# One-hot tiles with two tokens side by side instead of eight, in the dense expert weights of a two-model block

## The chip, the cores and the metric

The kernel runs on one core of a Trainium2 chip. The metric is the device time of one execution in microseconds. The kernel before took 4570.91 us, the median of three runs (4564.49 to 4579.38).

## The reference

Two models run one after the other on 256 tokens of 1024 features. The first has two layers, and each layer ends in product-key experts (`_peer`); layer 0 runs them on two streams, the context and x, and layer 1 on x alone. For one token the experts are:

```
s      = query . keys, for 8 heads and two halves: 128 scores each
v, i   = top 16 of each half;  cand = the 16 x 16 sums;  sc, pos = top 16 of cand
g      = softmax(sc);  expert = i1 * 128 + i2
out    = sum over 8 heads x 16 ranks of g * gelu(h . U[expert]) * V[expert]
```

A token therefore chooses 128 of 16384 experts, and each choice has a first index i1 (0 to 127), a second index i2 (0 to 127) and a weight g. The second model (a gated delta rule layer, a sparse attention layer, memory attention and convolutional feed-forward) does not touch what is changed.

## The kernel before

The experts are computed densely: every expert for every token, with a weight that is zero where the expert was not chosen. The expert tables go by chunks of one first index, 128 chunks in each stream, and the 128 second indices of a chunk lie on partitions.

`peer` (from line 1201) runs two products per chunk. `first()` takes a chunk of U: a DMA into `raw`, a split into two float32r parts `whi` (ScalarE, line 335) and `wlo` (line 338, VectorE or GpSimd), 24 matmuls `ps_U` of 256 columns, and a gelu into a slot of the ring `A`. `second(c)` takes a chunk of V: the slot is split into `a_hi` and `a_lo` (lines 348 and 349), V is split in the same way, and 12 matmuls of 512 columns add to four banks `ps_acc`. U runs ahead of V by the slots of the ring.

Before `second` reads a slot it must be multiplied with the dense weights of that chunk, and this is the work that the change touches, `peer_weights` (from line 1158). One generator makes the weights of n first indices (36, then 46, then 46) for all 256 tokens of a stream, in 32 batches of TB = 8 tokens. A batch is:

- `P2` (line 1180, VectorE): a one-hot of i2 for each of the 128 choices on partitions, 128 columns for each of 8 tokens, float16
- `P1` (line 1183, VectorE): a one-hot of i1, n columns for each of 8 tokens
- `Pg` (line 1184, VectorE): P1 times the two float16 parts of g, both parts in one instruction
- `use` (line 1172, VectorE): the ring's slots times the products of the batch before
- 16 matmuls `ps_G` on TensorE (line 308 through `mm`), two for each token: the token's 128 columns of `P2` are the loaded weights, and the token's n columns of `Pg` are what moves through the array.

There are nine such generators: three ranges for each of the two streams of layer 0 and for the one stream of layer 1, so 288 batches and 4608 matmuls, 1536 of 36 columns and 3072 of 46. The first generator of a layer runs beside `first()` alone, while the ring fills, one chunk of U for each batch. The others run inside the loop over chunks of V, one or two batches in a pass, mostly beside a `first()` and a `second()`. In the last range of a layer U has ended, and a pass is a `second()` with its batches.

The low parts of the split weights go to VectorE or GpSimd by a counter: `pool_each` is 4 in the loop (every fourth on GpSimd), 1 (all on GpSimd) once U has ended and batches are still due, and 1 or 2 while the first generator runs. The order of instructions on each engine is made by the framework's scheduler; the 16 matmuls of a batch stay together. `P1`, `P2` and `Pg` have two buffers each. The tiles lie with the token as the innermost index, so one token's columns stand 8 float16 values apart:

```
P2 = pe.tile([P, P, TB], FH, tag="P2", bufs=2, name="P2")
self.mm(o, P2[:, :, half * HB + t], Pg[:, 0, :, half * HB + t], True, False)
self.mm(o, P2[:, :, half * HB + t], Pg[:, 1, :, half * HB + t], False, True)
```

Of the kernel before, what the change touches and what calls it, by code (L numbers as in the profile page):

```python
# [7 lines left out]
FT = mybir.dt.float32  # L8
FR = mybir.dt.float32r
FH = mybir.dt.float16  # L10
# [14 lines left out]
APART = 2             # layer 0's last tiles of the out-projection that do the context's half first  # L25
OUTB, OUTK = 3, 6     # first tiles of the out-projection that begin with the first OUTK chunks of y
MEMW = 3              # steps between a memory norm's squares and its sum
FRONTW = 5            # the same for the second stream's norm before the choice of experts
NK0 = 2               # steps of attention before the memory's products
GK = 2                # steps of memory attention before the out-projection  # L30
PE1 = range(40, 47)   # steps of the choice of experts beside which Pool makes all the low parts
# chunks whose squares Pool adds up before the sum over partitions, by norm
# [3 lines left out]
# ---------------------------------------------------------------- layout of the inputs (host)  # L36
def fm(a):
    """[T, D] -> [128, D/128, T], feature-major."""
    a = np.asarray(a)
    t, d = a.shape  # L40
    return np.ascontiguousarray(a.reshape(t, d // P, P).transpose(2, 1, 0))


def cols(v):
    """[n*128] -> [128, n]."""
    return np.ascontiguousarray(np.asarray(v).reshape(-1, P).T)


def pack_t(w):
    """[K, C] -> [C/128, 128, K/128 * 128]: column tiles, rows on partitions."""  # L50
    k, c = w.shape
    return np.ascontiguousarray(
        w.reshape(k // P, P, c // P, P).transpose(2, 1, 0, 3)).reshape(c // P, P, k)


def pack_m(w, g):
    """[K, C] -> [K/128/g, 128, g*C]: row chunks, all columns."""
    k, c = w.shape
    n = k // P // g
    return np.ascontiguousarray(w.reshape(n, g, P, c).transpose(0, 2, 1, 3)).reshape(n, P, g * c)  # L60
# [26 lines left out]
# column tiles of w_in, in the order of the array  # L87
T_G16, T_QK, T_V, T_GV, T_O, T_U, T_CV, T_FT, T_GATE = 0, 1, 5, 7, 9, 11, 13, 17, 19
EARLY = (T_G16, T_QK + 2, T_QK + 3, T_QK, T_QK + 1, T_CV + 2)   # the first tiles of w_in
ADA0 = (4, 0)     # the layers' first groups of 512 modulations that aren't made with the first norm  # L90
# [30 lines left out]
def sincos_parts():  # L121
    """Feature-major: half of the features depend on the row alone, half on the column alone."""
    e = fm(sincos())
    return np.ascontiguousarray(np.concatenate([e[:, :4, ::64].reshape(P, 16), e[:, 4:, :64].reshape(P, 256)], axis=1))


def constants():
    """Arrays that depend on shapes alone."""
# [25 lines left out]
    # slices of 40 columns: ones in column j; in columns 8 + j and 32 + j  # L154
# [34 lines left out]
def prep(I):  # L189
    """The arrays as the program reads them: reordered, and padded with zeros."""  # L190
# [14 lines left out]
    # the modulations of the first norm, chunk by chunk of its features: (chunk, half of the rows)  # L205
    A["wadaf"] = np.ascontiguousarray(
        I["w_ada"][0][:, :2 * D].reshape(2, 4, P, 2, KC, P).transpose(4, 0, 2, 1, 3, 5)).reshape(KC, 2, P, 1024)
    for l in range(2):
# [26 lines left out]
        # (branch, half of the columns): [row of 128, (column group, row group, column)]  # L235
# [33 lines left out]
    for i in range(2):  # L269
# [4 lines left out]
        A[f"wom{i}"] = np.ascontiguousarray(      # the memory's rows, two column tiles at a time  # L274
# [7 lines left out]
# ---------------------------------------------------------------- the program  # L282
class Kern:
    def __init__(self, tc, A, L, out):
# [8 lines left out]
        self.pool_each = 4     # GpSimd makes one of so many low parts  # L293
        self.n_ps = 0

    # ---- small things
# [13 lines left out]
    def tr(self, o, x):  # L310
        """o <- x transposed."""
# [17 lines left out]
    def split(self, raw, f=1024, own=None):  # L329
        """float32 -> two float32r parts whose sum it is, to float32's accuracy; own: a pool with tiles for them."""  # L330
# [10 lines left out]
    def weight(self, ap, f=1024, ahead=0, own=None):  # L341
        """ahead: by how many instructions it goes before its place in the program."""
# [3 lines left out]
    def hilo(self, hi, lo, src, copy=None):  # L346
        """hi, lo <- src; src float32 in SBUF."""
# [3 lines left out]
    # ---- constants  # L351
# [23 lines left out]
    def load_x(self, src_x, src_c):  # L375
# [4 lines left out]
        # the mixers' and experts' input: the context's tokens, then x's  # L380
# [15 lines left out]
    # ---- adaLN: mods[l][:, m*8+dc, stream]; streams: 0 the context, 1 x  # L396
    def ada_load_c(self):
# [3 lines left out]
        # silu(c) of both streams, in 32 columns  # L401
# [4 lines left out]
    def ada(self, l, g0, g1, pool):  # L406
        """Generator: column groups g0.. (of 512) of the modulations."""
# [15 lines left out]
    def first_chunks(self, Rs):  # L423
        """The first norm, chunk by chunk of the features as their modulations come, and with every chunk its part
        of the products with the first tiles of w_in, which are returned."""
# [39 lines left out]
    def ada_mm(self, ps, w, j, start, stop):  # L465
        """Each of the four products (half of the features, half of the columns) in its own columns of the array."""
# [15 lines left out]
    def gains(self, l, which):  # L482
        """gain * (1 + scale), for norm 1 or 2."""
# [7 lines left out]
    # ---- RMS norm over features, feature-major  # L491
    def squares(self, x, R=None, added=0):
        """The sum of so many chunks' squares, by GpSimd."""
# [12 lines left out]
    def rstd_bc(self, x, R=None, added=0, begun=False):  # L506
        """[128, NT] with 1/rms of each token in every row; begun: R is the sum of the squares of chunks."""
# [15 lines left out]
    def sqrt_ahead(self, at):  # L523
        """Has ACT load its table for sqrt, when at is there."""
# [3 lines left out]
    def rstd(self, R, ss, n):  # L528
        """R <- 1/sqrt(ss/n + eps)."""
# [3 lines left out]
    def norm(self, x, gain, shift, hi, lo, R=None, ks=range(KC), added=0):  # L533
        """hi, lo <- rmsnorm(x) * gain + shift; gain, shift: chunk -> [128, 1]."""
# [13 lines left out]
    # ---- products with streamed weights  # L548
    def lin_t(self, w, h, t0, t1, ps, nk=KC, k0=0, start=True, stop=True):
        """ps[:, :t1-t0] (+)= W^T h: the tile's 128 columns on partitions."""  # L550
# [7 lines left out]
    # ---- the mixer of the first model's layers  # L558
# [5 lines left out]
    def ctx_ahead(self):  # L564
        """Generator: the next layer's norm of the context, when its experts are done."""
# [6 lines left out]
    def mixer(self, l, side=()):  # L572
# [57 lines left out]
        def merge(i):  # L630
            """ysum += sigmoid(gate) * (z[i] @ w_branch[i]); after the last of them, the two parts of ysum in y."""
# [20 lines left out]
        # ---- mLSTM: gates, as rows in the order of the scan  # L652
        g16 = scratch("g16")[:, :2 * NT]
        nc.scalar.activation(g16, tile_of(T_G16, 0), AF.Identity, bias=lp("gateb"))
        # partitions: 64 * stream + 32 * direction + head
# [26 lines left out]
        # rows: 0 the exponents of the sources, 1 -m, 2 m0 - M (x), the sources' weights in the final state (context)  # L682
# [21 lines left out]
        # -M in two parts, its blocks of tokens 0, 0, 1, 1  # L704
# [4 lines left out]
        # ---- mLSTM: q, k (convolution over tokens, silu)  # L709
# [16 lines left out]
        # ---- mLSTM: v (with a column of ones), and the v of the spatial gating, token-major  # L726
# [30 lines left out]
        # ---- mLSTM: the two directions of every stream  # L757
# [6 lines left out]
        for s in (0, 1):  # L764
# [5 lines left out]
            for h in range(4):  # L770
# [26 lines left out]
                with tc.manual_schedule(engines={mybir.EngineType.PE}):  # L797
                    for d in range(2):
                        # block of targets: (column of Pt, block of sources)
# [5 lines left out]
        # norm over each head, output gate  # L805
# [20 lines left out]
        # ---- convolution branch: gate, and the convolution over tokens  # L826
# [13 lines left out]
        # ---- Fourier branch  # L840
# [5 lines left out]
        for s in streams:  # L846
            y1 = bp.tile([P, 2, 2, 2, P], FT, name="y1") if last else scratch("y1").rearrange(
                "p (b j c e) -> p b j c e", b=2, j=2, c=2)  # block, tile, cos|sin, channel
# [18 lines left out]
        # ---- convolution branch: the convolution over tokens  # L867
# [8 lines left out]
        # ---- spatial gating  # L876
# [42 lines left out]
        # ---- convolution branch  # L919
# [42 lines left out]
        # the last chunks of y come late  # L962
# [7 lines left out]
        # the context is finished first: its experts follow  # L970
# [12 lines left out]
    def ml_state(self, bp, qk, vx, rT, c0):  # L983
        """Final state of the context's scan, both directions: c0[(head%2, dk), dir, head, dv|1], zero in the rows of the other head."""
# [20 lines left out]
    def ml_out(self, bp, s, h, nd, qk, c0f, rT, hs):  # L1005
        """hs[:, block, head] <- the sum of both directions' outputs, token-major."""
        nc = self.nc
        # [token, (direction, block of tokens), dv|1]
# [25 lines left out]
    def advance(self, side, n=1):  # L1034
        """n steps of the generators in side."""
# [5 lines left out]
    # ---- product-key experts: every expert for every token, its weight zero where it isn't chosen  # L1041
    # first indices whose weights are made at a time, and slots of the ring, by the number of streams
    RANGES = {1: (36, 46, 46), 2: (36, 46, 46)}
    RING = {1: 77, 2: 66}
    TB = 8          # tokens in one batch of them
    GS = 16384.0     # the weights' scale in float16

    def peer_open(self, es, ngroups):
# [3 lines left out]
        self.io_t = self.pe.tile([P, P, self.TB], FH, name="io_t")  # L1052
        nc.vector.tensor_copy(self.io_t, iota.unsqueeze(2).broadcast_to([P, P, self.TB]))
# [9 lines left out]
    def peer_front(self, l, s, st):  # L1063
        """Generator: the chosen experts and their weights, slots (head, rank) on partitions."""
# [33 lines left out]
        gT = st["gT"] = pe.tile([P, 2, NT], FH, tag="gT", bufs=self.nh, name="gT")  # L1098
        for b in range(2):
# [43 lines left out]
            nc.scalar.copy(gT[:, 0, ts], ps[:, 2 * P:3 * P])  # L1143
            nc.vector.tensor_sub(gT[:, 1, ts], ps[:, 2 * P:3 * P], gT[:, 0, ts])
# [4 lines left out]
    def top16(self, s, v, i):  # L1149
        """v, i <- the 16 largest of s and their places, in order; s is overwritten."""  # L1150
# [7 lines left out]
    def peer_weights(self, st, A, s0, i0, n):  # L1158
        """Generator: the products of first indices i0..i0+n, in the slots of A from s0 on, times their weights."""
# [15 lines left out]

        for t0 in range(0, NT, TB):
            ts = slice(t0, t0 + TB)
            bc = lambda q, m: st[q][:, ts].unsqueeze(1).broadcast_to([P, m, TB])
            P2 = pe.tile([P, P, TB], FH, tag="P2", bufs=2, name="P2")
# [918 lines left out]
```

## Time and profile before

| What | Value |
|---|---|
| Median of three runs | 4570.91 us (4564.49 to 4579.38) |
| Profiled execution, span from first to last instruction | 4573.1 us; the profile gives no time of its own around the span |
| TensorE matmuls busy | 4452.0 us, 97% |
| VectorE busy | 3040.3 us, 66% |
| ScalarE busy | 2022.9 us, 44% |
| GpSimd busy | 1193.1 us, 26% |
| Mean granted TensorE clock | 0.981 of full speed |

Busy time counts an instruction from its start to its end, also while it is held up by another engine, so a busy VectorE may be waiting. Matmuls overlap: the time that one costs is the distance from its start to the next one's start, not its duration. A granted clock of 1.0 is 2.4 GHz, and 0.5 is 1.2 GHz.

### The profile page before, as it was taken

The numbers are of one execution on the slowest core, as the hardware profiler recorded it, in microseconds if no ns is written. First come the engines' busy times: TensorE is split into PE (matmuls) and PEld (weight loads), VectorE is DVE, ScalarE is ACT, GpSimd is POOL, SyncE is SP. The second block draws the span as 40 slices with busy tenths as digits, with TensorE's granted clock in tenths as the row PEclk, the third lists the DMA queues.
The fourth block names the chain that finished last, engine by engine and source line by source line (L and its number), as shares of the span: only waits on it lengthen the run. The fifth ranks groups of instructions, "written<-read, shape, count | busy, mean of one in ns | idle before, by whom it ended". The sixth has DMA issues, their size and how long they took to land. (4 is left out here: it accounts for less than half of the span.)

```text
span 4573.1 us, 79225 instructions
## 1 busy us (share of the span) xinstructions
PE 4452.0 (97%) x31661; PEld 4029.5 (88%) x31661; DVE 3040.3 (66%) x5528; ACT 2022.9 (44%) x3223; POOL 1193.1 (26%) x591
## 2 busy tenths in 40 slices
PE   8999999999999999999999999999999999999999
PEld 6777999899788888999888999899988889999899
DVE  5743698687765566564756758876757566686685
ACT  5343442534433335334245544334443464654454
POOL 1023354112211112112321234642134212222122
PEclk9999999999999999999999999999999999999999
DMA  5243453544545655446354444444544541456355
GB/s 195 95 159 116 135 160 112 177 130 152 180 164 182 219 184 160 139 135 188 107 170 146 146 153 158 137 144 143 170 157 134 189 141 33 146 185 196 111 167 157
DMA packets 192129, 693.89 MB, mean 152 GB/s; under 512 B 21640, under 2 KB 23312, under 8 KB 191760
## 3 DMA queue, kind: packets, MB, share of 16 engines
q1 hardware_dynamic: 191616, 688.31, 47.1%
q8 instruction: 248, 4.06, 0.4%
q14 instruction: 121, 0.99, 0.1%
q10 hardware_dynamic: 144, 0.52, 0.0%
HBM read 687.69 MB, written 1.06 MB: 151 GB/s over the span
## 5 line engine op out<-in xcount | busy, mean ns | idle before, releaser
L338 POOL TENSOR_TENSOR wlo<-raw,whi 128x1024 fp32r<-128x1024 f32 (+1 forms) x419 | 1034.0, 2469 | 2960.5 <-ACT whi L335 2766.1
L335 ACT CAST whi<-raw 128x1024 fp32r<-128x1024 f32 (+1 forms) x1190 | 1241.8, 1045 | 1192.9 <-PE ps_U L308 374.6
L338 DVE TENSOR_TENSOR wlo<-raw,whi 128x1024 fp32r<-128x1024 f32 (+1 forms) x771 | 958.4, 1244 | 506.0 <-ACT whi L335 494.2
L308 PE MATMUL ps_acc<-whi,a_hi 128*128 128x512 f32 x1536 | 642.5, 418 | 0.0
L308 PE MATMUL ps_acc<-wlo,a_hi 128*128 128x512 f32 x1536 | 625.4, 407 | 3.7 <-DVE wlo L338 2.5
L308 PE MATMUL ps_acc<-whi,a_lo 128*128 128x512 f32 x1536 | 621.1, 406 | 0.6 <-DVE a_lo L349 0.6
L308 PE MATMUL ps_U<-hh_hi,wlo 128*128 128x256 f32 x2048 | 579.9, 283 | 14.1 <-DVE wlo L338 11.7
L308 PE MATMUL ps_U<-hh_hi,whi 128*128 128x256 f32 x2048 | 581.3, 284 | 0.9 <-ACT whi L335 0.9
L308 PE MATMUL ps_U<-hh_lo,whi 128*128 128x256 f32 x2048 | 579.0, 283 | 0.0
L348 ACT CAST a_hi<-A 128x256 fp32r<-128x256 f32 x384 | 156.1, 407 | 863.7 <-PE ps_acc L308 847.7
L308 PE MATMUL ps_G<-Pg,P 128*128 128x46 f16 (+1 forms) x4608 | 425.5, 265 | 4.0 <-DVE Pg L1184 4.0
L349 DVE TENSOR_TENSOR a_lo<-A,a_hi 128x256 fp32r<-128x256 f32 x384 | 203.0, 529 | 335.3 <-ACT a_hi L348 333.0
L308 PEld LDWEIGHTS <-P 128*128 128x128 f16 x4608 | 385.9, 148 | 36.1 <-issue 19.1
L1180 DVE TENSOR_TENSOR P<-io_t,i2T 128x1024 f16<-128x1024 f16 x288 | 404.6, 1405 | 6.7 <-PE ps_G L308 6.7
L308 PEld LDWEIGHTS ps_U<-hh_hi,wlo 128*128 128x128 f32 x2048 | 389.4, 190 | 15.9 <-DVE wlo L338 13.3
L308 PEld LDWEIGHTS ps_U<-hh_hi,whi 128*128 128x128 f32 x2048 | 390.7, 191 | 10.1 <-ACT whi L335 1.1
L308 PEld LDWEIGHTS ps_U<-hh_lo,whi 128*128 128x128 f32 x2048 | 389.6, 190 | 8.4
L308 PEld LDWEIGHTS ps_acc<-whi,a_lo 128*128 128x128 f32 x1536 | 299.0, 195 | 73.0 <-DVE a_lo L349 1.1
L308 PEld LDWEIGHTS ps_acc<-whi,a_hi 128*128 128x128 f32 x1536 | 302.4, 197 | 67.9 <-issue 8.6
L308 PEld LDWEIGHTS ps_acc<-wlo,a_hi 128*128 128x128 f32 x1536 | 300.3, 195 | 65.7 <-DVE wlo L338 3.3
L308 PE MATMUL ps_U<-h_hi,wlo 128*128 128x256 f32 x1024 | 291.9, 285 | 10.0 <-DVE wlo L338 7.6
L308 PE MATMUL ps_U<-h_hi,whi 128*128 128x256 f32 x1024 | 294.6, 288 | 0.9 <-ACT whi L335 0.9
(610 smaller groups left out, 9305.1 us busy)
## 6 DMA issues: line engine op xcount, KB each, us to landing
raw<-in_U SPq DMA_DIRECT2D x384, 512.0 KB, 3.7
raw<-in_V SPq DMA_DIRECT2D x384, 512.0 KB, 3.7
raw<-in_win SPq DMA_DIRECT2D x96, 512.0 KB, 3.8
raw<-in_wup SPq DMA_DIRECT2D x88, 512.0 KB, 3.8
raw<-in_wada SPq DMA_DIRECT2D x80, 512.0 KB, 4.5
raw<-in_wq SPq DMA_DIRECT2D x48, 512.0 KB, 3.7
raw<-in_gwin SPq DMA_DIRECT2D x37, 512.0 KB, 3.7
raw<-in_wdn SPq DMA_DIRECT2D x32, 512.0 KB, 4.4
```

What stands on the lines that cost most here:

```text
L308: self.nc.tensor.matmul(o, l, r, start=start, stop=stop)
L335: nc.scalar.copy(hi[:, :f], raw[:, :f])
L338: eng.tensor_sub(lo[:, :f], raw[:, :f], hi[:, :f].bitcast(FT))
L348: (copy or self.nc.scalar.copy)(hi, src)
L349: self.nc.vector.tensor_sub(lo, src, hi.bitcast(FT))
L1180: nc.vector.tensor_tensor(P2, self.io_t, bc("i2T", P), op=OP.is_equal)
```

## The change

The one-hot tiles keep their 8 tokens per batch, but they hold them as four groups of two: the group is the outermost index, then the 128 (or n) columns, then the two tokens (TQ = 2). One token's columns now stand 2 float16 values apart, for `P2` and for `Pg`. The constant `io_t` holds two copies of each number instead of eight and is read again for each group. The tile of g (`gT`) is laid out batch by batch so that it can be read in groups of two. `Pg` is made by two instructions, one for each part of g, instead of one. Number, order and sizes of the matmuls stay. Comments are removed throughout, without effect on the program.

```diff
     TB = 8
+    TQ = 2
-        self.io_t = self.pe.tile([P, P, self.TB], FH, name="io_t")
-        nc.vector.tensor_copy(self.io_t, iota.unsqueeze(2).broadcast_to([P, P, self.TB]))
+        self.io_t = self.pe.tile([P, P, self.TQ], FH, name="io_t")
+        nc.vector.tensor_copy(self.io_t, iota.unsqueeze(2).broadcast_to([P, P, self.TQ]))
...
-        gT = st["gT"] = pe.tile([P, 2, NT], FH, tag="gT", bufs=self.nh, name="gT")
+        gT = st["gT"] = pe.tile([P, NT // self.TB, 2, self.TB], FH, tag="gT", bufs=self.nh, name="gT")
...
-            nc.scalar.copy(gT[:, 0, ts], ps[:, 2 * P:3 * P])
-            nc.vector.tensor_sub(gT[:, 1, ts], ps[:, 2 * P:3 * P], gT[:, 0, ts])
+            tb = slice(b * P // self.TB, (b + 1) * P // self.TB)
+            gv = ps[:, 2 * P:3 * P].rearrange("p (k t) -> p k t", t=self.TB)
+            nc.scalar.copy(gT[:, tb, 0], gv)
+            nc.vector.tensor_sub(gT[:, tb, 1], gv, gT[:, tb, 0])
...
+        TQ = self.TQ
+        H = TB // TQ
         for t0 in range(0, NT, TB):
             ts = slice(t0, t0 + TB)
-            bc = lambda q, m: st[q][:, ts].unsqueeze(1).broadcast_to([P, m, TB])
-            P2 = pe.tile([P, P, TB], FH, tag="P2", bufs=2, name="P2")
-            nc.vector.tensor_tensor(P2, self.io_t, bc("i2T", P), op=OP.is_equal)
-            P1 = pe.tile([P, self.RG, TB], FH, tag="P1", bufs=2, name="P1")[:, :n]
-            Pg = pe.tile([P, 2, self.RG, TB], FH, tag="Pg", bufs=2, name="Pg")[:, :, :n]
-            nc.vector.tensor_tensor(P1, self.io_t[:, i0:i0 + n], bc("i1T", n), op=OP.is_equal)
-            nc.vector.tensor_tensor(Pg, P1.unsqueeze(1).broadcast_to([P, 2, n, TB]),
-                                    st["gT"][:, :, ts].unsqueeze(2).broadcast_to([P, 2, n, TB]), op=OP.mult)
+            bc = lambda q, m: (st[q][:, ts].rearrange("p (h t) -> p h t", h=H).unsqueeze(2)
+                               .broadcast_to([P, H, m, TQ]))
+            io = lambda j, m: self.io_t[:, j:j + m].unsqueeze(1).broadcast_to([P, H, m, TQ])
+            P2 = pe.tile([P, H, P, TQ], FH, tag="P2", bufs=2, name="P2")
+            nc.vector.tensor_tensor(P2, io(0, P), bc("i2T", P), op=OP.is_equal)
+            P1 = pe.tile([P, H, self.RG, TQ], FH, tag="P1", bufs=2, name="P1")[:, :, :n]
+            Pg = pe.tile([P, 2 * H, self.RG, TQ], FH, tag="Pg", bufs=2, name="Pg")[:, :, :n]
+            nc.vector.tensor_tensor(P1, io(i0, n), bc("i1T", n), op=OP.is_equal)
+            gt = st["gT"][:, t0 // TB].rearrange("p q (h t) -> p (q h) t", t=TQ)
+            for q in range(2):
+                nc.vector.tensor_tensor(Pg[:, q * H:(q + 1) * H], P1,
+                                        gt[:, q * H:(q + 1) * H].unsqueeze(2).broadcast_to([P, H, n, TQ]), op=OP.mult)
...
-                        self.mm(o, P2[:, :, half * HB + t], Pg[:, 0, :, half * HB + t], True, False)
-                        self.mm(o, P2[:, :, half * HB + t], Pg[:, 1, :, half * HB + t], False, True)
+                        h, q = divmod(half * HB + t, TQ)
+                        self.mm(o, P2[:, h, :, q], Pg[:, h, :, q], True, False)
+                        self.mm(o, P2[:, h, :, q], Pg[:, H + h, :, q], False, True)
```

## Rows read from the trace of the kernel before

**Rows 1.** First part of the page: busy time, share and instructions by engine.
```profile
PE 4452.0 (97%) x31661; PEld 4029.5 (88%) x31661; DVE 3040.3 (66%) x5528; ACT 2022.9 (44%) x3223; POOL 1193.1 (26%) x591
```

**Rows 2.** Busy time by stretch; columns are stretch, length, engines, granted clock, DMA.
```profile
880.00:1090.00 210.00, 210.00 (x1641) 197.58 (x1641) 163.80 (x452) 78.34 (x124) 37.03 (x14) 1.00 0.46 141
1240.00:1440.00 200.00, 200.00 (x1462) 174.56 (x1458) 122.79 (x207) 63.35 (x96) 26.41 (x11) 0.92 0.51 169
1560.00:1760.00 200.00, 200.00 (x1589) 178.39 (x1588) 141.17 (x244) 75.46 (x113) 33.57 (x14) 1.00 0.56 182
1840.00:2010.00 170.00, 170.00 (x1188) 154.91 (x1188) 107.73 (x192) 55.33 (x82) 25.40 (x11) 0.91 0.42 128
...
2890.00:3050.00 160.00, 152.36 (x1450) 150.78 (x1450) 133.56 (x144) 53.38 (x84) 90.96 (x38) 0.97 0.41 132
3050.00:3290.00 240.00, 239.36 (x1712) 218.75 (x1711) 161.83 (x258) 101.41 (x156) 47.52 (x24) 0.99 0.48 156
```

**Rows 3.** Groups by shape: the 46-column products of the one-hot tiles.
```profile
L308 PE MATMUL ps_G<-Pg,P 128*128 128x46 f16 x3072 | 301.2, 271 | 4.0 <-DVE Pg L1184 4.0
```

**Rows 4.** Timeline of TensorE's matmuls: start, duration (us), at three places.
```profile
1416.06 0.28 PE L308 MATMUL ps_U<-hh_hi,wlo 128*128 128x256 f32 x1
1416.18 0.28 PE L308 MATMUL ps_U<-hh_hi,whi 128*128 128x256 f32 x1
...
1419.33 1.65 PE L308 MATMUL ps_G<-Pg,P 128*128 128x46 f16 x16
1420.76 0.48 PE L308 MATMUL ps_acc<-whi,a_hi 128*128 128x512 f32 x1
...
2953.62 1.32 PE L308 MATMUL ps_G<-Pg,P 128*128 128x36 f16 x16
2954.74 0.37 PE L308 MATMUL ps_U<-h_hi,whi 128*128 128x256 f32 x1
```

**Rows 5.** Timeline of TensorE's weight loads: the first two of a batch.
```profile
1419.32 0.14 PEld L308 LDWEIGHTS <-P 128*128 128x128 f16 x1 [0.41 <-issue]
...
1419.36 0.23 PEld L308 LDWEIGHTS <-P 128*128 128x128 f16 x2
```

**Rows 6.** Timeline of TensorE around a fall of the granted clock.
```profile
1399.46 3.05 PE L308 MATMUL ps_G<-Pg,P 128*128 128x46 f16 x32
...
1402.87 0.63 PE L308 MATMUL ps_acc<-wlo,a_hi 128*128 128x512 f32 x1
1403.29 0.63 PE L308 MATMUL ps_acc<-whi,a_lo 128*128 128x512 f32 x1
```

**Rows 7.** Timeline of GpSimd and VectorE while the ring fills, layer 1.
```profile
2954.88 2.40 POOL L338 TENSOR_TENSOR wlo<-raw,whi 128x1024 fp32r<-128x1024 f32 x1 [1.65 <-ACT whi L335]
2955.35 2.47 DVE L1180 TENSOR_TENSOR P<-io_t,i2T 128x1024 f16<-128x1024 f16 x1
...
2958.93 2.39 POOL L338 TENSOR_TENSOR wlo<-raw,whi 128x1024 fp32r<-128x1024 f32 x1 [1.66 <-ACT whi L335]
```

**Rows 8.** Timeline of GpSimd and VectorE after U has ended, layer 1.
```profile
3445.28 2.40 POOL L338 TENSOR_TENSOR wlo<-raw,whi 128x1024 fp32r<-128x1024 f32 x1 [1.90 <-ACT whi L335]
...
3448.99 0.42 DVE L349 TENSOR_TENSOR a_lo<-A,a_hi 128x256 fp32r<-128x256 f32 x1
...
3449.57 2.40 POOL L338 TENSOR_TENSOR wlo<-raw,whi 128x1024 fp32r<-128x1024 f32 x1 [1.88 <-ACT whi L335]
```

**Rows 9.** VectorE's instructions by line: duration in ns, min/median/max, then first and last start.
```profile
L1180 DVE TENSOR_TENSOR P<-io_t,i2T x288: 675/685/2748, 648.8 to 3510.5; 128x1024 f16<-128x1024 f16 x144
L1183 DVE TENSOR_TENSOR P<-io_t,i1T x288: 293/337/2559, 651.0 to 3504.8; 128x368 f16<-128x368 f16 x96, 128x288 f16<-128x288 f16 x48
L1184 DVE TENSOR_TENSOR Pg<-P,gT x288: 443/528/2753, 657.5 to 3512.6; 128x736 f16<-128x736 f16 x96, 128x576 f16<-128x576 f16 x48
...
L1104 DVE TENSOR_TENSOR cand<-vt x24: 672/684/2904, 530.4 to 2865.6; 128x512 f32<-128x512 f32 x24
...
L1125 DVE TENSOR_TENSOR eq<-eq,itf x24: 1200/1221/3436, 613.0 to 2905.5; 128x1024 f16<-128x1024 f16 x24
```

## The prediction

> **What bounds the kernel.** I read the busy shares first: TensorE is at 97% and no other engine above 66% [rows 1], so time is won where TensorE's work shrinks, as long as nothing else is full there. The second view is the table of stretches that hold the generators of expert weights [rows 2]: in the four stretches from 880 to 2010 us TensorE is busy all the time, in the one from 3050 for 239 of 240 us, and VectorE for 63 to 78% of each. Third is the timeline of TensorE's starts, since the distance from start to start is what a matmul costs [rows 4]. Sixteen products of 46 columns go from 1419.33 to 1420.76, 89 ns each, 3072 of them busy for 301 us in all [rows 3]; sixteen of 36 columns from 2953.62 to 2954.74, 70 ns each. Both are 1.94 ns for a column, so it is the moving columns that set the pace and not the weight load, which has 128 columns in either case. The float32r products of 256 columns next to them start 0.12 us apart, 0.47 ns a column [rows 4]. What differs is the distance of columns in memory: 16 bytes for the one-hot tiles, 4 bytes for float32r.
>
> **TensorE.** After the change a token's columns stand 4 bytes apart, like those of float32r. If the pace follows the distance, 46 columns take 46 x 0.47 = 22 ns and 36 take 17. Then the weight load is late next. The first two loads of a batch, which wait for no product, start 39 ns apart [rows 5]; that is with columns 16 bytes apart, so a load costs 39 ns or less. Bounds for a product are 22 ns (the load hides) and the present 89 and 70 (distance does not matter). I take 39, the only measured load. A batch of 46 columns falls from 1.43 to 0.62 us, one of 36 from 1.12 to 0.62: 0.81 and 0.50 us, or 26 and 16 us for a generator of 32 batches.
>
> The Trainium skill (TensorE: Matmul & The Clock Gate, Back-to-back issue gap) puts a stream of pairs of load and matmul at about 81 ns each at 128 columns; as a floor here it would leave 8 ns on the 46-column products and nothing on the others, some 20 us in all. The trace disagrees with it as a floor, for the 36-column pairs already run at 70 ns [rows 4].
>
> **The clock.** The granted clock is 0.92 from 1240 to 1440, 0.91 from 1840 to 2010 and 0.99 from 3050 to 3290 [rows 2]. At one of these falls 32 one-hot products had run for 2.8 us, and the 512-column products behind them start 0.42 us apart [rows 6], 1.2 GHz in place of 2.4. In the stretch from 1560, where the batches have 36 columns, the clock stays at 1.00. After the change even two batches are 1.3 us, little more than the 1.12 of one batch there, so I expect the falls to go: 0.08 x 200 + 0.09 x 170 + 0.01 x 240 = 34 us. At worst they stay and this is nothing.
>
> **VectorE.** Elements stay the same in number; Pg becomes two instructions of the size of P1. That is 2 x 337 against 528 ns [rows 9], 0.15 us more for a batch and 5 us for a generator. What I can't read from a row is an input whose rows hold two float16 values, each row read 128 or n times. Lower bound: 685 ns for P2 as now. Upper bound: the 1221 ns that L1125 takes for as many float16 values where one input repeats single values, one element at a time instead of two [rows 9]. I take no loss, because the nearest row is L1104: it rereads one 4-byte value sixteen times, and 512 of them take 684 ns [rows 9], just what the 512 pairs of P2 take now; a repeated word by itself is not slow.
>
> The Trainium skill speaks against the change here: Vector Engine (DVE) Microarchitecture Reference, section Measured stream behaviour on trn2, says that a port streams at full rate only where its elements come in runs of two or more adjacent 4-byte words (1.05 ns a column; 1.73 where one source hops at each). Two float16 values are one word, so by it P2 would be some 0.35 us longer, an estimate, and a batch 0.72. By L1104, which stays on a word at full rate, this is no hop, and no run here shows the other reading.
>
> **Stretch by stretch.** In the five with U and V, TensorE's saving counts while VectorE still fits:
> - from 880: 26 us; VectorE would have 164 + 5 of 184 us, 92%, and some passes will wait: I count 22
> - from 1240: 26 + 16 for the clock = 42; VectorE 128 of 158
> - from 1560: 16; VectorE 146 of 184
> - from 1840: 26 + 15 = 41; VectorE 112 of 129, so 40
> - from 3050: 26 + 2 = 28; VectorE 167 of 212.
>
> That is 148 us. The other four generators gain little, since there GpSimd makes all low parts, and VectorE's one-hots stand still while it does: P2 takes 2.47 us beside a low part of 2.40 and ends 0.54 after it [rows 7], not its own 0.69. While the ring fills a pass is 4.05 us, from low part to low part [rows 7]. What can't overlap is 2.40 + 0.54 + P1 and Pg at 36 columns (about 0.29 and 0.44, the minima of rows 9) + 0.15 for the split = 3.82. So at most 0.2 us x 64 batches = 13 us is to be had of the 32 that TensorE gives; I take 6. After U has ended a pass is 4.29 us, and the same sum with 46 columns and a_lo (0.42) is 2.40 + 0.54 + 0.34 + 0.53 + 0.15 + 0.42 = 4.38 [rows 8, 9]: nothing gained, at worst 0.1 us x 62 batches = 6 lost. The shorter io_t and the regrouped gT are a handful of instructions outside the loops; nothing.
>
> Sum: 148 + 6 = 154 us. The profiled span is 4573.1 us, 2 us above the median, with nothing recorded around it; 4573 - 154 = 4419, and against the median 4417.
>
> **Rivals.**
> 1. *The load shortens too.* Rows 5 bound it from above only; with columns closer it may reach 25 ns. Another 14 ns x 16 x 160 batches in the five stretches is 36 us, of which VectorE, near 90% in two of them, leaves 25: 4392.
> 2. *GpSimd holds VectorE up.* GpSimd makes every fourth low part in the five stretches too, and holds up VectorE as in rows 7. For it: VectorE at 87 to 92% after the change. Against it: busy time already includes its waits. With half of everything kept, 77 us: 4494.
> 3. *VectorE drops to one element at a time* (slower). If rows of two values don't pair, P2 costs 0.54 us more, P1 0.19 and Pg 0.38, with the split 1.26 us a batch. While the ring fills the sum becomes 4.93 against 4.05, 56 us for 64 batches; after U has ended 5.49 against 4.29, 1.2 x 62 = 74. In the five stretches VectorE then has 204, 163, 181, 143 and 202 us, and the gains shrink to 6, 37, 16, 27 and 28 = 114. Net 16 slower at least, 4587; with the waits of an engine at its limit about 30, 4600. It decides from about 1.15 us more per batch on; below that the kernel is still faster. For it: no row shows an input in rows of two. Against it: L1104 as above.
> By the Trainium skill's rates, as above, the loss would be 0.87 us a batch with the split and the kernel still faster, about 4515, an estimate.
> 4. *The distance is not it* and the pace stays. Then the split alone costs, 9 us where VectorE bounds: 4580. Against it: 1.94 ns a column has no other difference to stand on but the type, and float16 is the narrower one.
>
> **How the numbers follow.** Forecast 0.52 (own range 4395 to 4450), rivals 0.17, 0.15, 0.10 and 0.06. The range takes in the first rival's centre and the second's, 4380 to 4510. What this kernel's measurement can tell from no change is 0.3%, 14 us. Faster 0.52 + 0.17 + 0.15 + 0.02 (the third rival where its price stays under 1.15 us) = 0.86; same 0.05, from the fourth; slower 0.09.
>
> **What would show it.** Sixteen one-hot products from start to the next engine work in 0.6 to 0.7 us, equal for 36 and 46 columns if the load is the bound, and in proportion if not. P2's shortest duration at 0.68 us, half a Pg at 0.34; 1.2 and 0.53 would be rival 3. Granted clock 1.00 in the stretches from 1240 and 1840. Passes of some 3.9 us while the ring fills and 4.3 after U. The forecast is wrong if products still cost 70 ns or more, if VectorE's shares in the five stretches reach 97%, or if the clock falls as often as before.

## The result and the profile after

The changed kernel takes 4386.5 us (median of 4 runs, 4381.2 to 4392.3) against 4567.7 for the kernel before beside it (4558.1 to 4579.4): ratio 0.9608, 95% interval 0.9588 to 0.9628, 181 us faster. The forecast was 4417, its range 4380 to 4510, of which it gave 4395 to 4450 to its own mechanism; the time lies outside that inner range and nearest to the first rival's 4392.

First part of the page of the changed kernel, by engine, to be held against [rows 1]: TensorE is busy for 246 us less, VectorE for 66 more.

```profile
PE 4205.9 (96%) x31661; PEld 3765.4 (86%) x31661; DVE 3106.5 (71%) x5816; ACT 2021.7 (46%) x3223; POOL 1225.9 (28%) x591
```

Groups by shape of the changed kernel, the one-hot products (busy us, mean ns of one, then idle time before them and who ended it). In [rows 3] one took 271 ns and TensorE waited 4 us for `Pg`; now one takes 185 or 180 ns, and TensorE waits 54 us for `Pg` (36.1 + 17.6).

```profile
L308 PE MATMUL ps_G<-Pg,P 128*128 128x46 f16 x3072 | 114.0, 185 | 39.2 <-DVE Pg L1193 36.1 <-ACT a_hi L348 0.4
L308 PE MATMUL ps_G<-Pg,P 128*128 128x36 f16 x1536 | 61.6, 180 | 19.0 <-DVE Pg L1193 17.6
```

TensorE's starts in the changed kernel, two batches of 46 columns and one of 36, each with the work behind it; they answer to [rows 4].

```profile
1259.16 0.98 PE L308 MATMUL ps_G<-Pg,P 128*128 128x46 f16 x32
1259.98 0.47 PE L308 MATMUL ps_acc<-whi,a_hi 128*128 128x512 f32 x1
...
2844.21 0.75 PE L308 MATMUL ps_G<-Pg,P 128*128 128x36 f16 x16
2845.14 0.39 PE L308 MATMUL ps_U<-h_hi,whi 128*128 128x256 f32 x1 [0.18 <-DVE A L1175]
```

Thirty-two products now take 0.82 us, 25.6 ns each. From one start to the next the median is 25 ns for 36 and for 46 columns (71 and 90 before). The second place shows what is late next: the product behind the batch waits 0.18 us for VectorE.

VectorE's instructions by line in the changed kernel (ns, min/median/max), against [rows 9]: `P2` and `P1` have their old medians and, within 11 ns, their old minima; a half of `Pg` is as long as a `P1`.

```profile
L1193 DVE TENSOR_TENSOR Pg<-P,gT x576: 294/337/2559, 655.7 to 3336.8; 128x368 f16<-128x368 f16 x126, 128x288 f16<-128x288 f16 x66
L1187 DVE TENSOR_TENSOR P<-io_t,i2T x288: 664/684/2879, 650.3 to 3333.8; 128x1024 f16<-128x1024 f16 x144
L1190 DVE TENSOR_TENSOR P<-io_t,i1T x288: 295/337/2557, 651.5 to 3329.0; 128x368 f16<-128x368 f16 x96, 128x288 f16<-128x288 f16 x48
```

Busy time by stretch of the changed kernel, columns as in [rows 2], one row for each of the nine generators.

```profile
700.00:805.00 105.00, 86.66 (x997) 82.18 (x997) 93.20 (x152) 27.95 (x42) 52.63 (x22) 0.89 0.31 102
920.00:1063.00 143.00, 140.81 (x1367) 130.26 (x1366) 140.06 (x413) 60.09 (x96) 41.04 (x11) 1.00 0.50 158
1259.00:1381.00 122.00, 120.99 (x1243) 104.03 (x1238) 111.53 (x218) 47.26 (x72) 22.89 (x8) 1.00 0.61 207
1500.00:1677.00 177.00, 177.00 (x1592) 155.29 (x1592) 147.41 (x273) 74.42 (x112) 33.63 (x13) 1.00 0.61 198
1791.00:1902.00 111.00, 110.88 (x1119) 100.84 (x1116) 109.14 (x230) 46.11 (x69) 23.20 (x8) 1.00 0.51 164
2065.00:2166.00 101.00, 79.54 (x722) 57.06 (x721) 92.35 (x166) 25.23 (x36) 44.73 (x18) 0.88 0.31 95
2779.00:2900.00 121.00, 115.21 (x1251) 106.46 (x1251) 119.43 (x150) 41.66 (x63) 79.78 (x32) 1.00 0.41 136
2934.00:3114.00 180.00, 176.90 (x1523) 159.07 (x1522) 158.51 (x274) 86.63 (x135) 45.86 (x21) 0.99 0.53 178
3216.00:3338.00 122.00, 105.48 (x844) 77.58 (x840) 118.83 (x177) 39.01 (x58) 68.94 (x29) 0.97 0.38 125
```

Three things are to be seen. In the stretches from 1259 and 1791 the granted clock is 1.00, where it was 0.92 and 0.91. In those from 920 and 1791 VectorE is busy for 98%. And in the first, sixth and ninth row (a ring fill, and the two after U has ended) TensorE idles for 18, 21 and 17 us, in the first two at a clock of 0.89 and 0.88 (1.00 and 0.92 before): here the gain went.

The time by generator, from the first start of its products to the last, read from the two timelines:

| Stretch (after) | Before, us | After, us | Saved | Forecast |
|---|---|---|---|---|
| 700, ring fills, layer 0 | 94.6 | 104.6 | -10.0 | 6 with the next fill |
| 920 | 171.5 | 142.9 | 28.6 | 22 |
| 1259 | 165.6 | 121.7 | 43.9 | 42 |
| 1500 (36 columns) | 198.9 | 176.4 | 22.5 | 16 |
| 1791 | 156.5 | 111.1 | 45.4 | 40 |
| 2065, U ended, layer 0 | 108.2 | 100.3 | 7.9 | 0 |
| 2779, ring fills, layer 1 | 126.7 | 121.2 | 5.5 | see above |
| 2934 | 209.8 | 179.6 | 30.2 | 28 |
| 3216, U ended, layer 1 | 129.1 | 121.9 | 7.2 | 0 |
| Sum | | | 181.2 | 154 |

### The profile page after: what moved, and what is told of

It is laid out like the page before. It is cut to its first block, busy times and chain, and to the rows that moved or that the text cites. A ratio compares the mean times of both kernels' runs of the same rounds, so it can differ in the third digit from the quotient of the medians.

```text
span 4390.5 us, 79517 instructions
## 1 busy us (share of the span) xinstructions
PE 4205.9 (96%) x31661; PEld 3765.4 (86%) x31661; DVE 3106.5 (71%) x5816; ACT 2021.7 (46%) x3223; POOL 1225.9 (28%) x591
## 5 line engine op out<-in xcount | busy, mean ns | idle before, releaser
L338 POOL TENSOR_TENSOR wlo<-raw,whi 128x1024 fp32r<-128x1024 f32 (+1 forms) x419 | 1068.7, 2552 | 2746.8 <-ACT whi L335 2504.1
L308 PE MATMUL ps_acc<-whi,a_hi 128*128 128x512 f32 x1536 | 629.7, 410 | 0.0
L308 PE MATMUL ps_acc<-wlo,a_hi 128*128 128x512 f32 x1536 | 614.0, 400 | 6.8 <-DVE wlo L338 4.4
L308 PE MATMUL ps_acc<-whi,a_lo 128*128 128x512 f32 x1536 | 609.2, 399 | 0.0
L308 PEld LDWEIGHTS ps_acc<-whi,a_hi 128*128 128x128 f32 x1536 | 291.9, 190 | 65.3 <-issue 9.1
L1193 DVE TENSOR_TENSOR Pg<-P,gT 128x368 f16<-128x368 f16 (+1 forms) x576 | 339.2, 627 | 0.0
L1187 DVE TENSOR_TENSOR P<-io_t,i2T 128x1024 f16<-128x1024 f16 x288 | 308.0, 1070 | 4.6 <-PE ps_G L308 4.6
L308 PE MATMUL ps_U<-h_lo,whi 128*128 128x256 f32 x1024 | 292.1, 285 | 0.0
```

The costliest lines, as they stand in the source:

```text
L308: self.nc.tensor.matmul(o, l, r, start=start, stop=stop)
L338: eng.tensor_sub(lo[:, :f], raw[:, :f], hi[:, :f].bitcast(FT))
L1187: nc.vector.tensor_tensor(P2, io(0, P), bc("i2T", P), op=OP.is_equal)
L1193: nc.vector.tensor_tensor(Pg[:, q * H:(q + 1) * H], P1, gt[:, q * H:(q + 1) * H].unsqueeze(2).broadcast_to([P, H, n, TQ]), op=OP.mult)
```

## The experiments

Ten kernels ran, each beside the kernel before (median 4571.0 in the first four, 4565.5 in the next four, 4568.9 in the last two). The ns given for a product below are medians from the start of one product to the start of the next.

### One operand at a time

**pg_only**: the loaded weights go back to eight tokens side by side (16 bytes apart), the moving columns stay at two tokens.

```diff
-            P2 = pe.tile([P, H, P, TQ], FH, tag="P2", bufs=2, name="P2")
+            P2 = pe.tile([P, P, TB], FH, tag="P2", bufs=2, name="P2")
...
-                        self.mm(o, P2[:, h, :, q], Pg[:, h, :, q], True, False)
+                        self.mm(o, P2[:, :, half * HB + t], Pg[:, h, :, q], True, False)
...
```

> The changed kernel with P2 (what is loaded) back at eight tokens side by side, Pg (what moves) left at two, and still two instructions for Pg. Theory A, load and moving each cost by the distance of their own columns, and a product takes the longest of load, moving and a fixed step of 25 ns: the load alone sets the pace at 39 ns, the gap of the first two loads before the change, for 36 and 46 columns alike. Against the changed kernel 14 ns x 4608 = 65 us of TensorE's time come back, of which VectorE's limit hides some 25: ratio to before 0.965 to 0.972. Rival B, only the moving columns mattered and the load was never in the way: 25 ns and 0.961.

Measured: 4465.9 us, ratio 0.9772 (0.9751 to 0.9793). TensorE's starts in this kernel:

```profile
1304.13 2.14 PE L308 MATMUL ps_G<-Pg,P 128*128 128x46 f16 x32
1306.11 0.48 PE L308 MATMUL ps_acc<-whi,a_hi 128*128 128x512 f32 x1
...
2840.39 1.16 PE L308 MATMUL ps_G<-Pg,P 128*128 128x36 f16 x16
2841.40 0.36 PE L308 MATMUL ps_U<-h_hi,whi 128*128 128x256 f32 x1
```

60 ns for both shapes. Equal paces for 46 and 36 columns mean that the load sets them, as the forecast had it; but a load of 16-byte steps is 60 ns in a stream, not the 39 that lie between the first two (39 here too), and so the kernel is slower than the expected 0.965 to 0.972. Why the first two are closer was not found out.

**p2_only**: the reverse, the loaded weights at two tokens, the moving columns at eight (with `Pg` in one instruction).

```diff
-            Pg = pe.tile([P, 2 * H, self.RG, TQ], FH, tag="Pg", bufs=2, name="Pg")[:, :, :n]
+            Pg = pe.tile([P, 2, self.RG, TB], FH, tag="Pg", bufs=2, name="Pg")[:, :, :n]
...
-                        self.mm(o, P2[:, h, :, q], Pg[:, h, :, q], True, False)
+                        self.mm(o, P2[:, h, :, q], Pg[:, 0, :, half * HB + t], True, False)
...
```

> The changed kernel with Pg (what moves) back at eight tokens side by side and in one instruction, P2 (what is loaded) left at two. Theory A: the moving columns set the pace as before, 89 and 70 ns, the gap of the first two loads falls to 15 ns without use, the clock falls as often as before from 1240 to 1440 us: ratio to before 0.995 to 1.003. Rival C, the load sets the pace: 25 ns and about 0.96.

Measured: 4538.0 us, ratio 0.9924 (0.9898 to 0.9949).

```profile
1299.16 2.88 PE L308 MATMUL ps_G<-Pg,P 128*128 128x46 f16 x32
1301.83 0.48 PE L308 MATMUL ps_acc<-whi,a_hi 128*128 128x512 f32 x1
...
2904.29 1.25 PE L308 MATMUL ps_G<-Pg,P 128*128 128x36 f16 x16
2905.34 0.36 PE L308 MATMUL ps_U<-h_hi,whi 128*128 128x256 f32 x1
```

2.67 us for 32 products and 1.05 for 16; the medians are 85 and 68 ns, nearly in proportion to the columns. The moving operand was the bound, and a shorter load alone is worth 33 us, more than the expected 0.995 to 1.003 allowed. Two things were not in the expectation. The products became 5 and 3 ns shorter, some 20 us in all (an estimate), so that a product is not quite the longest of load and moving alone. And the fifth generator ran at a clock of 0.98 in place of 0.90 and saved 13.5 us; in the third it stayed at 0.91, as expected. Both operands alone give 105 + 33 = 138 us, both together 181: each takes away what the other leaves as the bound.

### Other distances

**tq4**: four tokens side by side, 8 bytes from column to column. **tq1**: one, 2 bytes.

```diff
-    TQ = 2
+    TQ = 4   # tq1: TQ = 1
```

> The changed kernel with four tokens side by side (TQ = 4), columns 8 bytes apart in both tiles. Theory A with a cost in proportion to the distance: 1.94 x 8/16 = 0.97 ns a column, 45 ns for 46 columns and 35 for 36, ratio to before 0.968 to 0.975. Rival D, a distance below 16 bytes is free: 25 ns for both shapes, ratio 0.961. VectorE's instructions keep their durations in both.

> The changed kernel with one token for itself (TQ = 1), columns 2 bytes apart in both tiles. Of the 25 ns for a product in the changed kernel: if they are a fixed step of a pair of load and product they stay 25 with columns closer still; if they are the load or the moving at 4 bytes they fall. VectorE then reads the indices one value at a time: P2 1.2 us in place of 0.68, P1 0.53 and each Pg 0.53 in place of 0.34, 1.1 us more for a batch, so VectorE bounds everywhere: ratio to before 0.99 to 1.03. If VectorE kept its two elements at a time, 0.961.

Measured: tq4 4436.4 us, ratio 0.9706 (0.9685 to 0.9727); tq1 4626.8, ratio 1.0116 (1.0092 to 1.0140). TensorE's starts in tq4:

```profile
1300.47 1.65 PE L308 MATMUL ps_G<-Pg,P 128*128 128x46 f16 x32
1301.95 0.47 PE L308 MATMUL ps_acc<-whi,a_hi 128*128 128x512 f32 x1
```

1.48 us for 32: 46 ns, and 37 for 36 columns, about 1.0 ns a column: half the distance, half the price. In tq1 the products start 25 ns apart, as in the changed kernel, so 25 ns is a step that neither columns nor distance shorten. VectorE's lines in tq1:

```profile
L1193 DVE TENSOR_TENSOR Pg<-P,gT x576: 443/529/2755, 658.1 to 3575.9; 128x368 f16<-128x368 f16 x126, 128x288 f16<-128x288 f16 x66
L1187 DVE TENSOR_TENSOR P<-io_t,i2T x288: 1197/1214/3434, 652.0 to 3571.6; 128x1024 f16<-128x1024 f16 x144
L1190 DVE TENSOR_TENSOR P<-io_t,i1T x288: 443/529/2711, 653.7 to 3572.8; 128x368 f16<-128x368 f16 x96, 128x288 f16<-128x288 f16 x48
```

Single values nearly halve VectorE's rate, to the 1.2 us for `P2` that the forecast's third rival took from L1125 [rows 9], and the kernel is then 1.2% slower than before although TensorE's products are as short as they get. So that rival priced its mechanism fairly (0.4% slower by its sum, 0.6% with the waits). It had no term for the clock, whose mean fell from 0.981 to 0.966. Two tokens are the least that keeps VectorE at two elements at a time.

### The split of Pg

**split_only**: the kernel before with `Pg` in two instructions.

```diff
-            nc.vector.tensor_tensor(Pg, P1.unsqueeze(1).broadcast_to([P, 2, n, TB]),
-                                    st["gT"][:, :, ts].unsqueeze(2).broadcast_to([P, 2, n, TB]), op=OP.mult)
+            for q in range(2):
+                nc.vector.tensor_tensor(Pg[:, q], P1,
+                                        st["gT"][:, q, ts].unsqueeze(1).broadcast_to([P, n, TB]), op=OP.mult)
```

> The kernel before with Pg alone changed: two instructions of a half each in place of one, the one-hot tiles still eight tokens side by side. What is asked: the price of the split by itself. Theory A (0.15 us a batch, only where VectorE bounds): in the ring fill and after U has ended, 126 batches, 10 to 19 us at most, in the five other stretches nothing, since TensorE has 89 and 70 ns products to do; ratio 1.000 to 1.003. Rival: VectorE's share of 63 to 78% does not show how tight it is, and the split costs everywhere: 9 x 32 x 0.15 = 43 us, ratio about 1.009.

Measured: 4576.0 us over 12 runs, ratio 1.0015 (1.0002 to 1.0028): some 7 us by the ratio, in the theory's range, not the rival's. Where it falls is not shown: the ring fills stay at 94.5 and 126.7 us, and the two generators that grew by some 5 us or more (171.5 to 177.4 and 108.2 to 113.1) did so at a lower clock (1.00 to 0.96 and 0.92 to 0.86).

### GpSimd's low parts

The changed kernel's gain stopped where GpSimd makes all low parts. Three kernels take them away there, one takes them out of the five stretches with U and V too, and one makes the edits of both_dve to the kernel before.

```diff
+        self.pool_each = 1 << 30          # fill_dve, both_dve, before_both, loop_dve
         for k, _ in enumerate(gens[0]):
...
-                    self.pool_each = 1 if pos["u"] == total else 4
+                    self.pool_each = 1 << 30 if pos["u"] == total else 4    # end_dve, both_dve, before_both
+                    self.pool_each = 1 << 30                                # loop_dve
```

> The changed kernel, but while the ring fills (both layers) no low part is made on GpSimd; VectorE makes them all. Theory A: while the ring fills a pass of 3.96 us (layer 1) is GpSimd's low part, with VectorE's one-hots held up beside it. Without it VectorE has for a batch 0.42 (A) + 0.42 (a_lo) + 0.68 + 0.30 + 2 x 0.30 us and what is left of its share of other work, about 3.3 to 3.5 us: some 0.5 us x 62 batches = 20 to 30 us less than the changed kernel; ratio to the kernel before 0.954 to 0.957. Rival: VectorE's own work fills the pass (GpSimd only takes work off it) and the low parts come on top, 0.4 us x 62 = 25 us more: ratio about 0.966.

> The changed kernel, but in the last two generator stretches of each layer, after U has ended, no low part is made on GpSimd (before: all). Theory A: the passes of 4.1 us there are GpSimd's (2.47 us, in which VectorE's P2 stands still, then P2's rest, P1, Pg); without it a pass is VectorE's sum of about 3.5 us or less: 0.3 to 0.5 us x 62 = 15 to 30 us less than the changed kernel; ratio to the kernel before 0.954 to 0.958. Rival: VectorE bounds there with or without GpSimd, and no gain or a loss: ratio 0.960 to 0.966.

> Both of the last two edits together: GpSimd makes low parts only between the ring's fill and the end of U. Theory A: the gains add, since the stretches are apart: 35 to 60 us less than the changed kernel, ratio to the kernel before 0.947 to 0.953. Rival (VectorE bounds either way): ratio 0.960 or above.

| Kernel | Median, us | Ratio to before (95%) | Fill L0 | U ended L0 | Fill L1 | U ended L1 |
|---|---|---|---|---|---|---|
| before | 4567.7 | 1 | 94.6 | 108.2 | 126.7 | 129.1 |
| before_both | 4560.7 | 0.9978 (0.9965 to 0.9990) | 94.5 | 103.3 | 126.7 | 129.1 |
| changed | 4386.5 | 0.9608 (0.9588 to 0.9628) | 104.6 | 100.3 | 121.2 | 121.9 |
| fill_dve | 4337.4 | 0.9497 (0.9478 to 0.9516) | 72.3 | 98.7 | 103.9 | 122.1 |
| end_dve | 4341.0 | 0.9505 (0.9483 to 0.9526) | 103.8 | 79.2 | 121.2 | 97.3 |
| both_dve | 4295.2 | 0.9400 (0.9381 to 0.9420) | 72.3 | 80.2 | 103.9 | 97.4 |

All three gains are larger than expected, and they add: 49 + 45 = 94 us alone, 91 together. Why is seen in one pass while the ring fills in layer 1. VectorE in the changed kernel (start, duration):

```profile
2840.68 0.45 DVE L1175 SCALAR_TENSOR_TENSOR A<-A,ps_G 128x288 f32<-128x288 f32 x1
2841.04 0.69 DVE L1187 TENSOR_TENSOR P<-io_t,i2T 128x1024 f16<-128x1024 f16 x1
2841.65 2.73 DVE L1193 TENSOR_TENSOR Pg<-P,gT 128x288 f16<-128x288 f16 x2
2844.41 0.31 DVE L1190 TENSOR_TENSOR P<-io_t,i1T 128x288 f16<-128x288 f16 x1
2844.64 0.45 DVE L1175 SCALAR_TENSOR_TENSOR A<-A,ps_G 128x288 f32<-128x288 f32 x1
```

GpSimd beside it:

```profile
2841.43 2.56 POOL L338 TENSOR_TENSOR wlo<-raw,whi 128x1024 fp32r<-128x1024 f32 x1 [1.39 <-ACT whi L335]
```

And VectorE in fill_dve, where it makes the low part itself:

```profile
2791.93 0.46 DVE L1175 SCALAR_TENSOR_TENSOR A<-A,ps_G 128x288 f32<-128x288 f32 x1 [0.49 <-PE ps_G L308]
2792.30 0.68 DVE L1187 TENSOR_TENSOR P<-io_t,i2T 128x1024 f16<-128x1024 f16 x1
2792.90 0.52 DVE L1193 TENSOR_TENSOR Pg<-P,gT 128x288 f16<-128x288 f16 x2
2793.34 1.22 DVE L338 TENSOR_TENSOR wlo<-raw,whi 128x1024 fp32r<-128x1024 f32 x1
2794.48 0.30 DVE L1190 TENSOR_TENSOR P<-io_t,i1T 128x288 f16<-128x288 f16 x1
2795.27 0.46 DVE L1175 SCALAR_TENSOR_TENSOR A<-A,ps_G 128x288 f32<-128x288 f32 x1 [0.49 <-PE ps_G L308]
```

Two halves of `Pg` that take 0.52 us by themselves take 2.73 beside the low part. VectorE loses 2.2 us to an instruction that costs it 1.22 (the expectations put that at 0.42, too low), and the pass falls from 3.96 to 3.34 us, with VectorE now waiting for TensorE.

> The kernel before (one-hot tiles of eight tokens) with the two edits to GpSimd: no low part on GpSimd while the ring fills or after U has ended. Theory A: in the changed kernel TensorE's saving in these stretches was real but had no effect, because GpSimd's low part set the pass; with the old products TensorE itself takes as long as GpSimd. In the changed kernel with both edits TensorE is busy for 72 of 72, 69 of 80, 104 of 104 and 97 of 97 us there; the old products add 32 x (1.12 - 0.40) = 23 us to each fill and 32 x (1.43 - 0.40) = 33 us to each of the others, which gives 95, 112, 127 and 130 us, against 94.6, 108.2, 126.7 and 129.1 in the kernel before: no gain, ratio 0.997 to 1.003. Rival: the edits are worth their 90 us with either one-hot tiles: ratio about 0.980.

Measured: 0.9978 (table above): about 10 us, not 90. Busy time by stretch, first in this kernel, then in both_dve (ring fill of layer 0, U ended of layer 0, the same two of layer 1):

```profile
700.00:795.00 95.00, 95.00 (x998) 94.15 (x997) 71.80 (x142) 28.14 (x42) 1.36 (x1) 1.00 0.38 117
2195.00:2298.00 103.00, 101.81 (x714) 84.05 (x713) 77.94 (x151) 24.41 (x36) 0.00 (x0) 0.95 0.27 83
2908.00:3035.00 127.00, 127.00 (x1260) 125.70 (x1260) 86.45 (x155) 42.50 (x64) 0.00 (x0) 1.00 0.40 131
3384.00:3513.00 129.00, 129.00 (x849) 107.77 (x848) 95.21 (x173) 39.63 (x58) 0.00 (x0) 0.97 0.35 112
```

```profile
700.00:772.00 72.00, 72.00 (x989) 71.05 (x986) 70.78 (x169) 27.58 (x42) 0.00 (x0) 1.00 0.44 140
2036.00:2116.00 80.00, 68.75 (x710) 50.83 (x709) 78.31 (x181) 23.69 (x36) 0.00 (x0) 0.98 0.35 106
2728.00:2832.00 104.00, 104.00 (x1248) 102.71 (x1245) 88.98 (x187) 41.75 (x63) 0.00 (x0) 1.00 0.49 159
3146.00:3243.00 97.00, 96.99 (x840) 73.45 (x837) 95.89 (x203) 38.44 (x58) 0.00 (x0) 1.00 0.46 148
```

With the old products TensorE is full without GpSimd too (127 of 127, 129 of 129), so the low parts cost nothing there. With the new ones the same edits are worth 91 us. In the kernel before, the two stretches of layer 1 stood at two limits of nearly the same height; the change took one away. After U has ended in layer 0 TensorE was busy for 103 of 108 us before, and the edits gave 5 us there.

> The changed kernel with both edits, and no low part on GpSimd in the five stretches with U and V either (before: every fourth). This tests the prediction's second rival at its own place. Rival 2 of the prediction (GpSimd holds VectorE up there): each of some 8 to 12 low parts of a stretch costs VectorE up to 2.0 us of standing still and would cost it 0.42 us itself: 5 to 10 us less in each of the three stretches where VectorE is busy for 98% (from 889, 1761 and, in part, 1229), ratio to the kernel before 0.933 to 0.938. Theory A: what VectorE loses there is hidden or as much as it would have to do itself: ratio 0.939 to 0.943.

Measured: 4283.3 us, ratio 0.9375 (0.9353 to 0.9397), 12 us under both_dve; the five stretches with U and V go from 142.9, 121.7, 176.4, 111.1 and 179.6 us in the changed kernel to 140.3, 119.8, 176.4, 110.5 and 174.1. In the first of them GpSimd still makes 6 of 43 low parts (11 before), in the others none. The ratio lies in the rival's range, but its interval reaches into that of theory A, and the three stretches that were to give 5 to 10 us each gave 2.6, 1.9 and 0.6; the most, 5.5 us, came where VectorE had been busy for 88%. So the forecast's second rival is at work, for some 11 us in place of 77. This is the fastest kernel of the study, 2.4% under the changed one.

## Why the forecast was right, and where it was off

**The direction and TensorE's mechanism: right.** The distance of columns in memory set the pace of the products. Undoing either operand brings a longer pace back, 60 ns for one and 85 for the other.

**The pace: the step that failed.** "I take 39, the only measured load" gave 39 ns a product; it is 25. The reading behind it was wrong the other way: with 16-byte steps a load in a stream costs 60 ns (pg_only), not "39 ns or less". The load is a price of the same 16-byte steps and fell with them, so 39 held as an upper bound for the new layout by luck, and as the centre it did not hold. The first rival had the pace of 25 ns, and nearly all of its 25 us more in the five stretches came true (171 saved, 148 forecast). With 25 the five terms would have been 33, 49, 23, 48 and 35 = 188 us (16 x 64 ns x 32 batches, or 16 x 45, with the clock's terms as they were); measured 171. Of the 17 us missing loop_dve gives back 11; the rest was not traced.

The Trainium skill (TensorE: Matmul & The Clock Gate, section Wait — 56ns, not 53.3ns?) states that starts never come closer than about 25 ns however few the columns. The trace agrees: 25 ns at 36 and 46 columns, 4 and 2 bytes apart, and no two of these products start closer in any run. The 81 ns for a pair, which the forecast weighed from the same page of the Trainium skill (section Back-to-back issue gap, for 128 columns), is not a floor here.

**The clock: right where it was forecast, and given back elsewhere.** The two stretches at 0.92 and 0.91 went to 1.00, and with the products these saved 44 and 45 us of 42 and 40. But falls came where TensorE now waits. TensorE in the changed kernel, ring fill of layer 0, where the clock was 1.00 before:

```profile
733.04 0.75 PE L308 MATMUL ps_G<-Pg,P 128*128 128x36 f16 x16 [3.24 <-DVE Pg L1193]
...
734.72 0.42 PE L308 MATMUL ps_U<-hh_hi,wlo 128*128 128x256 f32 x1
734.93 0.42 PE L308 MATMUL ps_U<-hh_hi,whi 128*128 128x256 f32 x1
```

The batch at 733.04 ends a wait of 3.24 us for `Pg`, and 1.7 us later the U products start 0.21 us apart, 1.2 GHz, in place of 0.12. Without the low parts on GpSimd (fill_dve) the waits are gone and the clock stays at 1.00. The forecast had no such term.

**VectorE's rate: right.** 684 ns for `P2` and 337 for half a `Pg`, as forecast; rows of two cost nothing, single values nearly double it (tq1). The Trainium skill's rule on runs of adjacent words (Vector Engine (DVE) Microarchitecture Reference, Measured stream behaviour on trn2), by which `P2` would be some 0.35 us longer, does not hold for this reread word: its minimum went from 675 to 664 ns. Two readings of the prediction are off without harm to the forecast: VectorE's shares in [rows 2] are 61 to 78%, not 63; and the third rival's 143 us for the stretch from 1840 adds the price of 28 batches where the others add 32, with which it is 148 and the rival's sum 21 us slower in place of 16.

**VectorE's room: a test that misled.** The forecast was to be wrong if VectorE's shares in the five stretches reached 97%. They reached 98% in those from 920 and 1791, and these still saved more than forecast, with TensorE busy for 141 of 143 and 111 of 111 us: busy time counts an instruction that GpSimd holds up, so the share says full before the engine is. In loop_dve VectorE makes all low parts of the stretch from 2934 (56 in place of 42) and is busy there for 147 us in place of 159.

**Ring fill: -4.5 us in place of 6.** In layer 1 the forecast's pass of 3.9 us is there (3.96) and saves 5.5. But the forecast priced all 64 batches by layer 1's pass of 4.05 us. In layer 0 only 20 chunks of U (480 products `ps_U`) run beside the 32 batches, not one for each, and the 94.6 us before were some 3.0 for a batch. There the stretch is 10.0 us longer, by the waits and the clock just shown; fill_dve, which takes the low parts away, brings it to 72.3 us at a clock of 1.00. The low parts alone don't make it longer, though. This is the same stretch in pg_only, columns as in [rows 2]:

```profile
702.20:792.50 90.30, 90.30 (x994) 89.41 (x993) 88.78 (x152) 27.94 (x42) 51.28 (x22) 1.00 0.39 119
```

With the same 22 instructions on GpSimd and products of 60 ns TensorE never idles, the clock stays at 1.00, and the stretch is 14 us shorter than with products of 25 ns. So it takes both, the low parts on GpSimd and products short enough for TensorE to run out of work; how the waits and the falls of the clock feed each other was not traced.

**After U has ended: 15 us in place of 0.** The forecast took the 4.29 us pass [rows 8] for VectorE's sum. In layer 1 it was TensorE's, here in the kernel before:

```profile
3445.28 0.48 PE L308 MATMUL ps_acc<-whi,a_hi 128*128 128x512 f32 x1
...
3448.16 1.62 PE L308 MATMUL ps_G<-Pg,P 128*128 128x46 f16 x16
3449.56 0.48 PE L308 MATMUL ps_acc<-whi,a_hi 128*128 128x512 f32 x1
```

From 3445.28 on twelve V products take 2.88 us and the batch behind them 1.40, 4.28 without a gap, and before_both stays at 129.1 us without any low part. After the change VectorE sets the pass, with `P2` held up by the low part to 2.44 to 2.51 us, at 4.05 to 4.12 us (its instructions `A` start at 3280.62, 3284.67 and 3288.79). In layer 0 only 17 passes of V go with the 32 batches, 28 in layer 1, so of the forecast's 62 passes of 4.29 us there were at most 28. The forecast's sum of 4.38 was too long since it added whole durations, while VectorE's instructions start 0.08 to 0.09 us before the one ahead of them ends (2841.04 + 0.69 against 2841.65 in the pass above).

## What to carry to other kernels

Before a matmul's pace is put down to its columns, compare its ns per column with that of another shape in the same trace: where it is several times longer, look at how far apart both operands' elements lie, and price each operand's new pace, not only the moving one. Where a change takes work off the bounding engine, ask in each stretch what the second limit is, and whether work that was handed to a helper engine is now that limit: handing it back was worth 91 us after the change and 10 before it.

## What was not expected of the hardware

- The distance of the elements sets the price of both operands: a weight load of 128 columns takes 60 ns in a stream at 16 bytes, and at 4 bytes no more than 25; moving columns take 1.94 ns each at 16 bytes (1.85 to 1.89 beside a load at 4 bytes), 1.0 at 8.
- At 4 and 2 bytes 25 ns remain, for 36 and 46 columns alike.
- A low part on GpSimd (2.4 us) holds VectorE's one-hots for 1.8 to 2.2 us, more than the 1.22 us in which VectorE makes that low part itself.
